# A two-layer trunk on one core: weights split in half tiles, and the first S5 scan issued behind the first SSD chunk

## The chip, the core and the metric

The kernel runs on one core of a Trainium2 chip. The metric is the device time of one execution in microseconds (us). The core has a matrix engine (TensorE, PE in the profile), three engines that work on tiles (VectorE or DVE, ScalarE or ACT, GpSimd or POOL), and SyncE (SP), whose queue issues all of this kernel's transfers. Tiles lie in SBUF with 128 partitions; matmuls write to PSUM. The three runs of the kernel before took 910.59, 910.69 and 911.84 us; the median is 910.69.

## The reference

The reference is a trunk of two layers on a sequence of 512 rows with 1024 columns, in fp32. Layer 0 runs two mixers side by side, and their inputs come from one projection:

```
hn = rmsnorm(h, layer_norm_w[i])
p = h @ w_in                       # gate S5 | gate SSD | S5 input u | SSD x,B,C | SSD dt
y_a = s5_mixer(u, ...)  * silu(z_a)
y_b = rmsnorm(ssd_mixer(xbc, dt, ...) * silu(z_b), ssd_norm_w, SSD_GROUPS)
h = h + concat(y_a, y_b) @ w_out
```

The S5 mixer is a diagonal complex state of 64 entries for each of 64 groups of 16 channels, `x_t = A x_(t-1) + B u_t`, with `y = C x + D u`, a GELU and a GLU. The SSD mixer has a causal depthwise convolution of width 4 over x, B and C, a SiLU, and then a chunked scan with chunks of 128 rows: within a chunk `y_diag = (C B^T * decay) (x dt)`, between chunks a state for each head that is carried on with a decay, and `y_off` from the carried state. Layer 1 is a chunkwise retention with four heads (q, k, v, gate), a group norm and an output projection. At the end stands an RMSNorm.

## The kernel before

**Projections.** Activations lie transposed, as eight tiles of 128x512 (eight slices of the 1024 inputs). A product with a weight tile of 128x1024 gives 128 output columns for all 512 rows. `ld_w` (L95) loads such a tile with one transfer into a `raw` buffer (three of them), and `split_w` (L101) makes two tiles of it: ACT copies it in a rounded form to `wh` (L107), and DVE subtracts that from the raw tile to `wl`, the low part (L108). There are two buffers each of `wh` and `wl`. In the trace the tile of a weight `z0` is called z0w when raw, z0h and z0l when split. `mm3` (L111) sums three products for each of the eight slices: high part by high input (L115), high part by low input (L116), low part by high input (L117), 24 matmuls in all. Some early tiles are used unsplit: `ld_raw` (L203) puts them in turn in a buffer of `raw`, `wh` and `wl`.

**Layer 0.** Its stages are x (SSD projection and conv), u (S5 input projection), z (gate projection), s (an SSD chunk: decays, states), t (the outputs of that chunk), and for the S5 mixer, in four parts j: l (load), g (state tables), a (scan), b (kernel tables), k (taps), c (outputs). The string `ORDER` (L36) sets the order in which these are written, and with it the priority of their instructions. A scheduler then orders each engine's queue by priority and readiness; weight splits (`rank_w`) and steps that free a PSUM bank (`rank_e`) have ranks of their own, and `tc.issue_after(x)` keeps an instruction behind x.

- The conv of tile m takes the PSUM sum of its projection through an ACT copy (L354) and three DVE steps (L357, tile cva), then a SiLU on ACT (L359). The last DVE step frees the PSUM bank, of which there are three for projections.
- The S5 input: ACT writes u to the tile us (L275), SP stores it to DRAM as `u_d` (L278), and `s5_load` reads two such tiles back in another layout as U (L730). The two of part 1 are us2 and us3, and U1 is read from them.
- A scan, `s5_scan`: PE forms the input sums S from the tables tm and al and from U (L755); DVE multiplies them by the rotation table rot (L767, L768, to the tiles gi and X), adds (L770), scans (L772), rotates back (L775, L777) and adds again (L782, to X and mg). rot is built by POOL (L534 to L539).
- Kernel tables, `s5_kern`: POOL multiplies and adds the tables O (L798, L802), and SP stores them to `o_d` (L803). Taps, `s5_taps`: PE forms K, ACT copies it to ks (L817), and DVE adds the feed-through on 16 columns for each half (L819).
- Outputs, `s5_out`: PE sums Y from Or (O read back) by X (L844) and from T (ks read back) by U (L845).
- An SSD chunk c with its two groups, `ssd`: transposes px, DVE products xdt (L385) and xds (L390), PE states st, DVE yos (L399) from the carried state, and the decays dec: read back from DRAM (L402), ACT Abs (L405) and Exp (L406), DVE product (L407). `ssd_y` uses yos, dec and xdt on PE (L425, L428).
- The gates z are stored to DRAM and read back later (zb2r is such a tile); the first group-norm sum over them is rsg0ps (L168).

**Layer 1** is made of projections by `ld_w` and `mm3` (or the same three products with the weights as moving operand, for v), and of the retention steps between.

## Time and profile before

| | |
|---|---|
| median of three runs | 910.69 us |
| the profiled execution | 915.33 us |
| its span in the trace | 913.6 us |
| mean granted clock of PE | 0.975 |
| PE busy | 868.6 us (95%) |
| DVE busy | 542.5 us (59%) |
| ACT busy | 359.5 us (39%) |
| POOL busy | 229.3 us (25%) |

The profiled execution is 4.64 us longer than the median. An engine's share of the span is a mean over both layers; layer 0 takes the first half of the span, layer 1 the second. In the trace's timeline a row has the start and the length of an instruction, or of several of one kind in a row, the engine, the line and the tiles, and in brackets the idle time just before it and what ended it. A row with `SPq` is SP issuing a transfer. The granted clock is given as a share of 2.4 GHz.

### The profile page before, as it was taken

Reading aid. Unit: us, or ns where it says so; the run is one execution under the profiler, and the core shown is the slowest. Engines: PE = TensorE matmul, PEld = TensorE weight load, DVE = VectorE, ACT = ScalarE, POOL = GpSimd, SP = SyncE. Lnnn points to the kernel's source line nnn. Section 1 sums busy time; section 2 is a strip of 40 time slices with the busy share of each in tenths; the row PEclk is TensorE's granted clock in tenths of the full one; section 3 lists DMA queues with packets and bytes.
Section 4 is the critical chain, followed back from the end, with each engine's and each line's share of the span. In section 5 each row is a group of like instructions: output and inputs, shape, how many; then the busy total and the mean of one; then the engine's idle time right before and its main releaser. Section 6 shows DMA issues by size and latency. Waiting matters only on the chain.

```text
span 913.6 us, 11520 instructions
## 1 busy us (share of the span) xinstructions
PE 868.6 (95%) x4348; PEld 683.1 (75%) x4348; DVE 542.5 (59%) x922; ACT 359.5 (39%) x572; POOL 229.3 (25%) x187
## 2 busy tenths in 40 slices
PE   8999955989989899999999999999999999999996
PEld 4345744757768787888888888888888888888885
DVE  6978769894883466453444544655633644448445
ACT  4323344425216444433434244345411244254432
POOL 0069997170572500000013122201000303110020
PEclk9999977979999899999999999999999999999999
DMA  7386313756549636773543221221332221222322
GB/s 244 122 223 210 106 51 119 204 161 205 148 124 323 215 104 190 255 238 107 208 141 112 93 93 47 93 92 47 99 103 99 93 91 47 93 70 70 116 70 93
DMA packets 64184, 121.45 MB, mean 133 GB/s; under 512 B 18112, under 2 KB 28672, under 8 KB 64000
## 3 DMA queue, kind: packets, MB, share of 16 engines
q1 hardware_dynamic: 64128, 120.71, 41.2%
q8 instruction: 34, 0.56, 0.2%
q14 instruction: 22, 0.18, 0.1%
HBM read 103.61 MB, written 17.07 MB: 132 GB/s over the span
## 4 chain that ended last, share of the span: by engine, by line
PE 68%; DVE 12%; POOL 8%; DMA 5%; SPq 2%; issue 2%; ACT 1%; ACTq 0%; POOLq 0%; DVEq 0%
PE g L115 3%; PE qk L117 3%; PE qk L116 3%; PE g L117 3%; PE g L116 3%; PE qk L115 3%; PE v L930 3%; PE v L931 3%; PE v L929 3%; PE gl L116 2%; PE gl L117 2%; PE gl L115 2%; PE out L117 2%; PE oa L116 2%; PE oa L117 2%
## 5 line engine op out<-in xcount | busy, mean ns | idle before, releaser
L903 POOL TENSOR_TENSOR rt<-rt,ru 128x512 f32<-128x512 f32 x16 | 27.2, 1721 | 134.7 <-DVE ru L902 134.7
L972 POOL TENSOR_TENSOR os<-os,os 128x512 f32<-128x512 f32 x12 | 15.5, 1292 | 139.8 <-ACT os L970 106.9
L882 POOL TENSOR_TENSOR hs<-hs,hs 128x512 f32<-128x512 f32 x7 | 12.0, 1708 | 92.5 <-ACT hs L880 92.5
L798 POOL TENSOR_TENSOR O<-ct,s5pws 128x512 f32<-128x512 f32 x16 | 24.1, 1508 | 31.2 <-DMA ct<-in_s5c_dram 31.2
L405 ACT ACTIVATE dec<-dec,nacs 128x128 f32<-128x128 f32 x64 | 19.5, 388 | 29.3 <-DMA dec<-at_d 29.3
L902 DVE TENSOR_TENSOR ru<-qk,tab 128x512 f32<-128x512 f32 x16 | 10.9, 683 | 32.4 <-PE qk L117 32.4
L357 DVE SCALAR_TENSOR_TENSOR cva<-xbc,cvw,cva 128x511 f32<-128x511 f32 (+2 forms) x36 | 26.6, 740 | 4.3 <-ACT cva L354 4.0
L798 POOL TENSOR_TENSOR ot<-ct,s5pws 128x512 f32<-128x512 f32 x16 | 28.1, 1756 | 0.0
L802 POOL TENSOR_TENSOR O<-O,ot 128x512 f32<-128x512 f32 x16 | 27.3, 1736 | 0.0
L742 POOL TENSOR_TENSOR tm<-al,b 128x512 f32<-128x512 f32 x6 | 9.0, 1513 | 57.3 <-DMA b<-in_s5bP_dram 34.2
L461 POOL TENSOR_TENSOR za6r<-za6r,y 128x512 f32<-128x512 f32 x1 | 1.3, 1297 | 80.9 <-DMA h_d<-hb 80.9
L359 ACT ACTIVATE cva<-cva 128x512 f32<-128x512 f32 x12 | 7.6, 631 | 33.7 <-DVE cva L357 33.6
L1004 DVE TENSOR_TENSOR h<-h,out 128x512 f32<-128x512 f32 x8 | 5.5, 686 | 25.5 <-PE out L117 25.5
L1065 POOL TENSOR_TENSOR fin<-fin,fnw 128x512 f32<-128x512 f32 x4 | 5.1, 1301 | 58.7 <-ACT fq L1029 58.7
L535 POOL TENSOR_TENSOR s5rt<-rot,s5lv 128x512 f32<-128x512 f32 (+4 forms) x7 | 5.9, 837 | 50.7 <-DVE s5lv L677 50.7
L845 PE MATMUL Y<-T,U 128*64 128x128 f32 x128 | 17.4, 294 | 0.2 <-issue 0.2
L499 DVE TENSOR_TENSOR hb<-ob,hb 128x512 f32<-128x512 f32 x8 | 5.5, 689 | 20.1 <-PE ob L117 20.1
L528 DVE TENSOR_TENSOR h<-oa,h 128x512 f32<-128x512 f32 x8 | 5.5, 690 | 19.6 <-PE oa L117 19.6
L848 ACT ACTIVATE ysb<-Y 128x256 f32<-128x256 f32 x16 | 5.2, 379 | 30.2 <-PE Y L845 18.1
L844 PE MATMUL Y<-Or,X 128*64 128x128 f32 x64 | 13.7, 298 | 2.3 <-DMA Or<-o_d 2.3
L120 ACT ACTIVATE rh<-rt 128x512 fp32r<-128x512 f32 (+1 forms) x16 | 9.1, 577 | 16.9 <-POOL rt L903 16.9
L425 PE MATMUL y<-ident,yos 128*128 128x128 f32 x48 | 12.2, 339 | 3.8 <-DVE yos L399 3.8
(1726 smaller groups left out, 3012.4 us busy)
## 6 DMA issues: line engine op xcount, KB each, us to landing
al<-al_d SPq DMA_DIRECT2D x8, 512.0 KB
b<-in_s5bP_dram SPq DMA_DIRECT2D x8, 512.0 KB
dec<-at_d SPq DMA_DIRECT2D x8, 512.0 KB
o_d<-O SPq DMA_DIRECT2D x16, 256.0 KB
T<-kd SPq DMA_DIRECT2D x64, 64.0 KB
Or<-o_d SPq DMA_DIRECT2D x16, 256.0 KB
x<-in_xT_dram SPq DMA_DIRECT2D x8, 256.0 KB
u_d<-us SPq DMA_DIRECT2D x8, 256.0 KB
```

Source lines behind the costliest of these rows:

```text
L115: pe.matmul(ps, wh[:, k, :], xh[k], start=start and i == 0, stop=False)
L116: pe.matmul(ps, wh[:, k, :], xl[k], start=False, stop=False)
L117: pe.matmul(ps, wl[:, k, :], xh[k], start=False, stop=stop and i == len(ks) - 1)
L357: vec.scalar_tensor_tensor(g[:, d:], ps[:, 0:SEQ - d], cvw[:, m, j:j + 1], g[:, d:], op0=ALU.mult, op1=ALU.add)
L405: act.activation(dec[:, i, :], dec[:, i, :], AF.Abs, bias=nacs[:, c, 8 * gr + i:8 * gr + i + 1])
L798: pool.tensor_tensor(x.rearrange("p (g k c) -> p g k c", g=4, c=16), ct[:, c, par, 4 * hf:4 * hf + 4].unsqueeze(2).broadcast_to(sh), pws[: ...
L802: pool.tensor_tensor(o, o, tm, op=ALU.add)
L845: pe.matmul(dst, U[:, 8 * par + 4 * hf + i, :], Tp[hf][:, 2 * i + par, :], start=False, stop=True)
L903: pool.tensor_tensor(t1, t1, t2, op=op)
L929: pe.matmul(ps[c], hh[kk][:, cs], wh[:, i, :], start=kk == 0, stop=False)
L930: pe.matmul(ps[c], hh[kk][:, cs], wl[:, i, :], start=False, stop=False)
L931: pe.matmul(ps[c], hl[kk][:, cs], wh[:, i, :], start=False, stop=kk == KD - 1)
```

## The change

Four things are changed.

1. Split weights are kept as two half tiles of 128x512 each for the high and the low part (names with 0 and 1 at their end), with four buffers each in place of two whole ones. ACT and DVE split each half with an instruction of its own. `piece` picks the half for a slice. The early unsplit tiles that lie in `wh` or `wl` buffers come in two transfers of 256 KB. The v projection and the second `on` projection of layer 1 use the halves as lists, in hunks left out here.
2. In `ORDER`, the first scan (a0) stands behind the first SSD chunk (s0), and its products by rot are issued behind the chunk's second xds.
3. The Exp of the decays is issued behind the last conv SiLU.
4. In the taps, ACT copies only the columns from 16 on, and DVE's feed-through reads the first 16 from PSUM.

```diff
-ORDER = """d0 x8 x10 x9 e0 x11 q0 x0 b0 x1 x2 w0 l0 g0 x3 x4 x5 x6 k0 b1 a0 x7 g1 s0 u2 u3 l1 t0 s1 z0 a1 z1 k1 b2 t1 s2 u4 c0 u5
+ORDER = """d0 x8 x10 x9 e0 x11 q0 x0 b0 x1 x2 w0 l0 g0 x3 x4 x5 x6 k0 b1 x7 g1 s0 a0 u2 u3 l1 t0 s1 z0 a1 z1 k1 b2 t1 s2 u4 c0 u5
...
-        return split_w(raw, name, halves)
-
-    def split_w(raw, name, halves=1):
-        h = wq.tile([P, KD, P], F32R, name=name + "h", tag="wh", bufs=2)
-        lo = wq.tile([P, KD, P], F32R, name=name + "l", tag="wl", bufs=2)
-        n = KD // halves
+        return split_w(raw, name)
+
+    KH = KD // 2
+
+    def w_half(name, tag, dt):
+        return wq.tile([P, KH, P], dt, name=name, tag=tag, bufs=4)
+
+    def split_w(raw, name):
+        hs, ls = [], []
         with rank_w():
-            for k in range(0, KD, n):
-                act.activation(h[:, k:k + n], raw[:, k:k + n], AF.Copy)
-                vec.tensor_tensor(lo[:, k:k + n], raw[:, k:k + n], h[:, k:k + n].bitcast(F32), op=ALU.subtract)
-        return h, lo
+            for i in range(2):
+                h, lo = w_half(f"{name}h{i}", "wh", F32R), w_half(f"{name}l{i}", "wl", F32R)
+                src = raw[:, i * KH:(i + 1) * KH]
+                act.activation(h, src, AF.Copy)
+                vec.tensor_tensor(lo, src, h.bitcast(F32), op=ALU.subtract)
+                hs.append(h), ls.append(lo)
+        return hs, ls
+
+    def piece(w, k):
+        return w[k // KH][:, k % KH]
 
     def mm3(ps, w, xh, xl, ks=range(KD), start=True, stop=True):
         wh, wl = w
         ks = list(ks)
         for i, k in enumerate(ks):
-            pe.matmul(ps, wh[:, k, :], xh[k], start=start and i == 0, stop=False)
-            pe.matmul(ps, wh[:, k, :], xl[k], start=False, stop=False)
-            pe.matmul(ps, wl[:, k, :], xh[k], start=False, stop=stop and i == len(ks) - 1)
+            pe.matmul(ps, piece(wh, k), xh[k], start=start and i == 0, stop=False)
+            pe.matmul(ps, piece(wh, k), xl[k], start=False, stop=False)
+            pe.matmul(ps, piece(wl, k), xh[k], start=False, stop=stop and i == len(ks) - 1)
 
...
-            raw = (wp if tag == "raw" else wq).tile([P, KD, P], F32, name=name + "w", tag=tag, bufs=3 if tag == "raw" else 2)
             wcount[0] += 1
             with rank(tc.cur_priority - ahead):
-                wdma[name] = sp.dma_start(raw, src).ins
-            return raw
+                if tag == "raw":
+                    raw = wp.tile([P, KD, P], F32, name=name + "w", tag="raw", bufs=3)
+                    sp.dma_start(raw, src)
+                    return raw[:, 0:KH], raw[:, KH:KD]
+                halves = []
+                for i in range(2):
+                    halves.append(w_half(f"{name}w{i}", tag, F32))
+                    sp.dma_start(halves[i], src[:, i * KH:(i + 1) * KH])
+                return halves
 
         def mm1(ps, raw, x):
             for k in range(KD):
-                pe.matmul(ps, raw[:, k, :], x[k], start=k == 0, stop=k == KD - 1)
+                pe.matmul(ps, piece(raw, k), x[k], start=k == 0, stop=k == KD - 1)
...
-            act.activation(g, g, AF.Silu)
+            held["silu"] = act.activation(g, g, AF.Silu).ins
...
-                        vec.tensor_tensor(xds.rearrange("p (h d) -> p h d", d=64), ps_x.rearrange("p (h d) -> p h d", d=64),
-                                          ds[:, c, hs].unsqueeze(2).broadcast_to([P, 8, 64]), op=ALU.mult)
+                        s5.setdefault("fed", []).append(
+                            vec.tensor_tensor(xds.rearrange("p (h d) -> p h d", d=64), ps_x.rearrange("p (h d) -> p h d", d=64),
+                                              ds[:, c, hs].unsqueeze(2).broadcast_to([P, 8, 64]), op=ALU.mult).ins)
...
-                act.activation(dec, dec, AF.Exp, scale=-1.0)
+                with tc.issue_after(held["silu"]):
+                    act.activation(dec, dec, AF.Exp, scale=-1.0)
...
-            vec.tensor_tensor(gi[c][:, :, 1:], sc, rot[:, 0, g8, 1:], op=ALU.mult)
-            vec.tensor_tensor(gt[1 - c][:, :, 1:], sc, rot[:, 1, g8, 1:], op=ALU.mult)
+            with tc.issue_after(s5["fed"][1]):
+                vec.tensor_tensor(gi[c][:, :, 1:], sc, rot[:, 0, g8, 1:], op=ALU.mult)
+                vec.tensor_tensor(gt[1 - c][:, :, 1:], sc, rot[:, 1, g8, 1:], op=ALU.mult)
...
-        act.activation(ks.rearrange("p g l -> p (g l)"), ps_k[:, 0:256], AF.Copy)
+        pk = ps_k[:, 0:256].rearrange("p (g l) -> p g l", g=2)
+        act.activation(ks[:, :, 16:], pk[:, :, 16:], AF.Copy)
         for hf in range(2):
             vec.scalar_tensor_tensor(ks[:, hf, 0:16], s5["eye"], s5["dK"][:, 2 * j + hf:2 * j + hf + 1],
-                                     ks[:, hf, 0:16], op0=ALU.mult, op1=ALU.add)
+                                     pk[:, hf, 0:16], op0=ALU.mult, op1=ALU.add)
```

On DVE, around the first scan, the order before was this. The number after cva is the conv tile; in gi00 and X01 the first digit is the part, in xdt00, xds00 and dec00 the SSD chunk.

```order
L357 SCALAR_TENSOR_TENSOR cva6_895<-xbc6_864,cvw_225,cva6_895 128x510
L766 MEMSET gi00_986 128x8
L767 TENSOR_TENSOR gi00_986<-S00_949,rot_502 128x8x63
L768 TENSOR_TENSOR X01_989<-S00_949,rot_502 128x8x63
L766 MEMSET gi01_987 128x8
L745 TENSOR_TENSOR al10_1045<-al10_1045,b10_1046 128x512
L761 MEMSET mg0_983 128x8
L743 TENSOR_TENSOR tm10_1047<-tm10_1047 128x512
L745 TENSOR_TENSOR al10_1045<-al10_1045,b10_1046 128x512
L357 SCALAR_TENSOR_TENSOR cva6_895<-xbc6_864,cvw_225,cva6_895 128x509
L767 TENSOR_TENSOR gi01_987<-S01_950,rot_502 128x8x63
L768 TENSOR_TENSOR X00_988<-S01_950,rot_502 128x8x63
```

In the order after, these rows stand there; cva6 and the u3 splits stand ahead of them.

```order
L406 TENSOR_TENSOR xds00_1056<-px00_1050,dcd_241 128x512
L372 SCALAR_TENSOR_TENSOR cva7_1012<-xbc7_977,cvw_227,cva7_1012 128x511
L372 SCALAR_TENSOR_TENSOR cva7_1012<-xbc7_977,cvw_227,cva7_1012 128x510
L372 SCALAR_TENSOR_TENSOR cva7_1012<-xbc7_977,cvw_227,cva7_1012 128x509
L424 TENSOR_TENSOR dec00_1060<-dec00_1060,cbn0_1043 128x1024
L113 TENSOR_TENSOR z0l0_1333<-z0w_1330,z0h0_1332 128x512
L424 TENSOR_TENSOR dec01_1085<-dec01_1085,cbn0_1043 128x1024
L400 TENSOR_TENSOR xdt01_1074<-px01_1075,dtn_238 128x512
L113 TENSOR_TENSOR z0l1_1337<-z0w_1330,z0h1_1336 128x512
L406 TENSOR_TENSOR xds01_1081<-px01_1075,dcd_241 128x512
L785 TENSOR_TENSOR gi00_1136<-S00_1099,rot_510 128x8x63
L786 TENSOR_TENSOR X01_1139<-S00_1099,rot_510 128x8x63
```

The first scan product moved from in front of the last step of cva6 to behind cva7, the z0 splits and both groups of SSD chunk 0.

On SP, the transfers up to U1 were issued in this order before.

```order
L821 DMA kd_578<-ks0_918 256x1x128
L803 DMA o_d_615<-O100_925 128x512
L803 DMA o_d_615<-O101_931 128x512
L98 DMA u4w_1566<-in_w_u_dram 128x1024
L803 DMA o_d_615<-O110_937 128x512
L803 DMA o_d_615<-O111_943 128x512
L278 DMA u_d_229<-us2_1157 128x512
L98 DMA u5w_1684<-in_w_u_dram 128x1024
L278 DMA u_d_229<-us3_1191 128x512
L730 DMA U1_1194<-u_d_229 128x16x64
```

After, they stand like this.

```order
L840 DMA kd_586<-ks0_946 256x1x128
L755 DMA al11_1029<-al_d_489 128x1x1024
L756 DMA b11_1030<-in_s5bP_dram 128x1024
L98 DMA u4w_1614<-in_w_u_dram 128x1024
L821 DMA o_d_623<-O100_953 128x512
L821 DMA o_d_623<-O101_959 128x512
L821 DMA o_d_623<-O110_965 128x512
L821 DMA o_d_623<-O111_971 128x512
L293 DMA u_d_231<-us2_1193 128x512
L98 DMA u5w_1736<-in_w_u_dram 128x1024
L293 DMA u_d_231<-us3_1231 128x512
L747 DMA U1_1234<-u_d_231 128x16x64
```

The transfers from O100 to U1 kept their places among one another; u4w moved ahead of them, and the loads al11 and b11 stand behind the taps' store.

On PE, before, the outputs y11 of SSD chunk 1 stood among the first sums of u5.

```order
L844 MATMUL Y00_1627<-Or00_1599,X00_988 64x128
L845 MATMUL Y00_1627<-T00_1607,U0_729 64x128
L117 MATMUL u5_1683<-xh0_697,u5l_1687 128x512
L115 MATMUL u5_1683<-xh1_701,u5h_1686 128x512
L116 MATMUL u5_1683<-xl1_702,u5h_1686 128x512
L117 MATMUL u5_1683<-xh1_701,u5l_1687 128x512
L115 MATMUL u5_1683<-xh2_705,u5h_1686 128x512
L116 MATMUL u5_1683<-xl2_706,u5h_1686 128x512
L425 MATMUL y11_1481<-ident_82,yos11_1273 128x128
L428 MATMUL y11_1481<-dec11_1275,xdt11_1260 64x128 x2
```

After, y10 comes first behind the last sums of u5 and one of z2 on PE.

```order
L124 MATMUL u5_1735<-xh7_737,u5h1_1742 128x512
L409 MATMUL st11_1309<-xds11_1307,cbn1_1265 128x512
L412 MATMUL yo11_1311<-prev1_1097,cva11_369 128x512
L125 MATMUL u5_1735<-xl7_738,u5h1_1742 128x512
L126 MATMUL u5_1735<-xh7_737,u5l1_1743 128x512
L124 MATMUL z2_1882<-xh0_709,z2h0_1885 128x512
L442 MATMUL y10_1512<-ident_82,yos10_1284 128x128
L445 MATMUL y10_1512<-dec10_1286,xdt10_1271 64x128 x2
```

So all 24 sums of u5 moved in front of y10. Behind the rest of y10, PE goes on like this in the order after.

```order
L863 MATMUL Y00_1679<-Or00_1651,X00_1138 64x128
L864 MATMUL Y00_1679<-T00_1659,U0_741 64x128
L863 MATMUL Y00_1679<-Or01_1653,mg0_1133 64x128
L864 MATMUL Y00_1679<-T00_1659,U0_741 64x128
L863 MATMUL Y00_1679<-Or00_1651,X00_1138 64x128
L864 MATMUL Y00_1679<-T00_1659,U0_741 64x128
L442 MATMUL y11_1529<-ident_82,yos11_1313 128x128
L445 MATMUL y11_1529<-dec11_1315,xdt11_1300 64x128 x2
```

Four more sums of Y than before stand between y10 and y11, and 17 more sums of u5 and z2 stand ahead of y11.

## Rows read from the trace of the kernel before

**Rows 1.** Windows: start:end, length, busy us of PE, PEld, DVE, ACT, POOL, clock, DMA share, GB/s.

```profile
153.70:158.60 4.90, 4.88 (x12) 3.84 (x13) 4.82 (x6) 0.00 (x0) 1.09 (x1) 0.51 0.52 161
...
196.00:207.00 11.00, 10.79 (x64) 7.79 (x64) 9.26 (x14) 4.43 (x12) 2.79 (x2) 0.53 0.88 290
...
140.00:160.00 20.00, 10.16 (x35) 7.35 (x34) 19.83 (x17) 8.18 (x10) 14.71 (x8) 0.74 0.38 124
500.00:600.00 100.00, 100.00 (x473) 84.09 (x472) 50.89 (x88) 34.29 (x50) 19.29 (x13) 1.00 0.25 84
...
159.20:164.20 5.00, 5.00 (x45) 3.78 (x43) 3.03 (x6) 2.14 (x3) 0.00 (x0) 1.00 0.99 260
```

**Rows 2.** Waits of PE: what it waited for, us, times, longest.

```profile
PE z L117 <- DVE z0l L108: 7.8, 1, 7.8
...
PE u L115 <- DVE cva L357: 5.2, 1, 5.2
...
PE u L117 <- DVE u3l L108: 4.2, 1, 4.2
...
PE z L115 <- DVE cva L357: 2.1, 1, 2.1
```

**Rows 3.** Timeline of DVE: start, us, instruction, idle before it.

```profile
113.86 2.04 DVE L819 SCALAR_TENSOR_TENSOR ks<-eye,dK,ks 128x16 f32<-128x16 f32 x2
...
120.78 0.68 DVE L767 TENSOR_TENSOR gi<-S,rot 128x504 f32<-128x504 f32 x1 [4.21 <-POOL rot L536]
124.31 0.68 DVE L768 TENSOR_TENSOR X<-S,rot 128x504 f32<-128x504 f32 x1 [2.85 <-POOL rot L539]
...
128.82 0.73 DVE L357 SCALAR_TENSOR_TENSOR cva<-xbc,cvw,cva 128x509 f32<-128x509 f32 x1
...
151.49 2.17 DVE L108 TENSOR_TENSOR z0l<-z0w,z0h 128x1024 fp32r<-128x1024 f32 x1
...
168.92 0.69 DVE L385 TENSOR_TENSOR xdt<-px,dtn 128x512 f32<-128x512 f32 x1 [1.18 <-PE px L383]
...
194.35 0.69 DVE L399 TENSOR_TENSOR yos<-yo,dcd 128x512 f32<-128x512 f32 x1
...
341.48 0.38 DVE L819 SCALAR_TENSOR_TENSOR ks<-eye,dK,ks 128x16 f32<-128x16 f32 x2
```

**Rows 4.** Timeline of PE: u2's first and last sum, S10, y11, the group-norm sum.

```profile
118.74 0.48 PE L115 MATMUL u<-xh,u2h 128*128 128x512 f32 x1
...
124.06 0.39 PE L117 MATMUL u<-xh,u2l 128*128 128x512 f32 x1
...
166.87 0.68 PE L755 MATMUL S<-U,tm 128*64 128x64 f32 x8
...
195.10 0.49 PE L425 MATMUL y<-ident,yos 128*128 128x128 f32 x2 [3.75 <-DVE yos L399]
...
303.37 0.38 PE L168 MATMUL rsg0ps<-ones,zb2r 128*128 128x1 f32 x2 [2.41 <-ACT zb2r L475]
```

**Rows 5.** Timeline of ACT: us2.

```profile
140.49 0.57 ACT L275 ACTIVATE us<-u 128x512 f32<-128x512 f32 x1
```

**Rows 6.** Timeline of POOL: the last two adds of the tables O of part 1.

```profile
143.65 3.38 POOL L802 TENSOR_TENSOR O<-O,ot 128x512 f32<-128x512 f32 x2
```

**Rows 7.** Timeline of SP's queue: us2, us3, U1, and later zb2r.

```profile
147.47 0.38 SPq L278 DMA_DIRECT2D u_d<-us  x1
...
154.12 0.38 SPq L278 DMA_DIRECT2D u_d<-us  x1
158.15 0.37 SPq L730 DMA_DIRECT2D U<-u_d  x1
...
285.83 0.37 SPq L471 DMA_DIRECT2D zb2r<-z_d  x1
```

**Rows 8.** One line's instructions: min/median/max ns, first and last start; half and whole tile.

```profile
L121 DVE TENSOR_TENSOR xl<-xn,xh x8: 680/687/1639, 32.9 to 85.7; 128x512 fp32r<-128x512 f32 x8
...
L108 DVE TENSOR_TENSOR z3l<-z3w,z3h x1: 1224/1224/1224, 213.4 to 213.4; 128x1024 fp32r<-128x1024 f32 x1
```

More of the change, by code (lines that the diff above doesn't have):

```diff
@@ L93, in rank_e, with ld_w @@
         return rank(-1000000 + 20 * wcount[0])
-    def ld_w(src, name, halves=1, ahead=0):
+    def ld_w(src, name, ahead=0):
         raw = wp.tile([P, KD, P], F32, name=name + "w", tag="raw", bufs=3)
@@ L248, in layer0 @@
             for k in range(KD):
-                pe.matmul(pu[0], w0[0][:, k, :], xs[k], start=k == 0, stop=k == KD - 1)
+                pe.matmul(pu[0], piece(w0[0], k), xs[k], start=k == 0, stop=k == KD - 1)
             y0, last = root(sq[:1], D, "rs0"), held0[0]
@@ L1033, in layer1 @@
         for kq in range(4):
-            wh, wl = (q.rearrange("p k m -> p (k m)").rearrange("p (i n) -> p i n", n=512)
+            wh, wl = ([x.rearrange("p k m -> p (k m)") for x in q]
                       for q in ld_w(a["w_o1b"][0, kq].rearrange("p i (j m) -> p (i j) m", m=P), f"on{kq}"))
```

14 lines of the change are left out of this document (7 added, 7 removed).

## The prediction

> **What bounds the kernel now.** The windows come first: they show where TensorE (PE) is not working. From 500 to 600 us it is busy for all of the 100 us at full clock, with DVE at 51 and ACT at 34; from 140 to 160 it works for 10.16 of 20 us at a mean clock of 0.74, while DVE is busy for 19.83 [rows 1]. So layer 1 is limited by PE alone, and nothing that the change does to DVE, ACT or SP is worth anything there, as long as they stay under PE. What can be won lies in layer 0, where PE waits. The list of waits names its releasers there: z0's low-part weights 7.8 us, two conv results 5.2 and 2.1, u3's low part 4.2, together 19.3 us [rows 2].
>
> All four end on DVE, so DVE's own timeline is read next. DVE stood still for 4.21 us until 120.78 and for 2.85 more until 124.31, in front of the first scan's two products, which wait for a POOL table (rot) [rows 3]. In that queue stand, behind the products, the last conv tap of cva6 (128.82), which frees the PSUM bank that u3 wants, and, behind the whole scan, z0l at 151.49. The scan's output is not wanted by PE before the Y sums near 189. That is why PE stands: DVE spends 7.1 us idle and some 20 us on work that is early.
>
> **The order, part by part.** The scan moves behind the second xds of SSD chunk 0. By the order after, cva6, u3l, xdt00, xds00, cva7, dec00, z0l and dec01 all stand in front of the first scan product, and none of them reads the POOL table. POOL's table was complete when the 2.85 us wait ended at 124.31, and the sixteen or so DVE instructions that now stand ahead of the scan last beyond that, so no wait replaces the 7.1 us. The dec Exps wait for the last Silu; they are read by dec00's product only, and one table load instead of three is seen by ACT, which has idle time there. On ACT nothing that PE needs soon is queued behind that wait: z0h and us2 stand ahead of it or come while it is open. I take the four waits as gone except for about 2 us of z0's, so PE could reach its next fixed point, the first S sum of the second half (S10, 166.87 [rows 4]), 17.2 us earlier, at 149.7.
>
> **The wait that takes their place.** S10 reads U1, and U1 does not come earlier by as much. Its chain: us2 is ready on ACT at 141.06 (140.49 + 0.57) [rows 5], but its transfer stands on SP behind the four o_d transfers, and the last of those waits for POOL's add that ends at 147.03 (143.65 + 3.38) [rows 6]. So SP issued us2 at 147.47, then u5w, then us3 at 154.12, then U1 at 158.15, 4.03 us behind us3 [rows 7]. In the order after, the same chain stands on SP: O100 to O111, us2, u5w, us3, U1. What goes is the delay of us3 from 147.9 to 154.12, since u5w took a buffer that z0 held and no longer does. So us2 at 147.5, us3 at 148.3, U1 at 152.3. For its landing no row gives a time: between 4.0 (a transfer of half the size, us3, by U1's issue behind it) and 8.7 (S10 began so long after the issue without waiting). DMA carried nothing from 158 to 159 and then 260 GB/s for 5 us [rows 1], at which 0.5 MB with T's pieces behind it take some 3 to 4; I take 5, nearer to the first end. S10 then starts at 157.3 (156.3 to 161) in place of 166.87. (The Trainium skill, page "DMA: Bandwidth & Descriptors", section "Anatomy of one DMA — SWDGE (gpsimd) path", gives some 2.0 us fixed for each transfer and 436 GB/s on top: an estimate of 3.2 us for U1, by which S10 would start at 155.5 and 10.9 us would be won here. By that rule us3, of half the size, would need 2.6; the row's 4.03 says otherwise, and I stay with the row.) Two of the ten z1 sums that stood ahead now stand behind, 24 sums from 118.74 to 124.06 being 0.23 us apart [rows 4]: 0.46. Won at this place: 9.57 - 0.46 = **9.1 us**, of 17.2 removed; PE waits there for some 8 to 15 us.
>
> PE's clock: in 153.7 to 158.6, right after the 7.8 us wait, it was 0.51, and in 196 to 207, after a wait of 3.75, it was 0.53, so the lower of its two levels (1.2 GHz, not 2.4) nearly all along [rows 1]. After the new wait I expect a slow stretch of the same length: 4.9 x 0.49 = 2.4 at least, 5 at most (11 x 0.47, the other row); I take 2.8. Before paid one here too, but upstream of S10, inside the 166.87.
>
> **The next point, y11.** y11 started at 195.10, after waiting 3.75 us for yos11, which DVE began at 194.35 [rows 3, 4]. Before S10 to y11 is 28.2 us, 24.5 of it work. The order after puts 17 more projection sums ahead of y11 (16 of u5, one of z2: 3.9 us) and 4 more Y sums (0.4): the place that answers to 195.10 is 199.4. PE's side: 157.3 + 24.5 + 4.3 + 0.5 (z1) + 2.8 (clock) = 189.4. DVE's side: its xdt10 at 168.92 came 2.05 behind S10's start; at 157.3 + 2.05 + 1.0 for the slow clock it comes at 160.3, and the 25.4 us to yos11 carry over. Added: z2l and z3l's first half, 3 x 0.68 = 2.0 [rows 8], a product X that was earlier, 0.7; more slow PE sums that DVE waits for, 1.8; more time beside POOL, 1.5. Less: 1.7 for the taps (below). So yos11 begins at 190.0 to 192.6, say 191, and y11 0.75 behind it at 191.8: a wait of 2.4 us remains, and the gain is 199.4 - 191.8 = **7.6 us**. That wait is near the old one, so the slow stretch behind it is taken as unchanged.
>
> **The taps.** The two ks products took 2.04 us beside POOL (113.86) and 0.38 alone (341.48) [rows 3]. With K read from PSUM they have one SBUF tensor less. The conv taps, which also read PSUM, took 0.73 at 128.82 while POOL worked, so I take 0.38: 1.7 saved on DVE each time POOL works beside it, bounds 0 and 1.7 (at 0, yos11 and with it the end come 1.7 later). ACT's copy becomes shorter by 16 of 128 columns, worth nothing.
>
> **Half tiles.** A half takes 0.68 on DVE where a whole tile took 1.22 [rows 8]: 0.14 more a tile, and some more on ACT, which has more room. In layer 1 that lies under PE (51 of 100 us on DVE). In layer 0 ten tiles before y11 make 1.4 us on DVE, of which those in DVE's chain are in the sum already. PE may start on a first half some 0.7 us sooner where it waits for a low part; that is within the 2 us that I left of z0's. The early raw weights come in two transfers of half the size: one SP issue more each, about 0.35 by SP's rows [rows 7], hidden behind the transfers; bounds minus 0.5 and plus 0.5.
>
> **After y11.** The next waits of PE in layer 0 are short ones and are taken with their sizes, moved with everything else. The doubtful one is the first group-norm sum, 2.41: it began at 303.37 when ACT had zb2r [rows 4], a transfer that SP issued at 285.83 [rows 7], at the end of a chain of u, U and z_d transfers whose start is a scan on DVE. It moves only if that scan does.
>
> **Sum.** The profiled execution took 915.33 us, 4.64 above the median of 910.69; the terms are differences and so are carried to the median: 910.69 - 7.6 = **903.1**, I say 903.
>
> **Rivals.**
> A, the forecast: U1's arrival takes the place of the four waits, and half of the gain reaches the end. 900 to 906, chance 0.50.
>
> B, more: yos11 comes before PE does (DVE's collisions with POOL are smaller than I add, or U1 lands 1 us sooner), the wait at y11 goes, and with it the slow stretch behind, whose 11 us at 0.53 cost 5.2 [rows 1]. 7.6 + 5.2 gives 897.9; with the later waits shorter too, 894. For it: the margin is only 2.4 us. Against: U1's wait is as long a stop as the ones that go, and a stop has each time brought a slow clock. Chance 0.22.
>
> C, slower: the chain to zb2r does not move. By the order the first group-norm sum stands behind 16 of z8's 24 sums, where all of z8 and two of z9 were in front: 10 sums, 2.3 us, less work to fill the wait. If zb2r leaves ACT no sooner than before, just ahead of 303.37 in the profiled time, PE arrives 7.6 us early, waits, and starts all that follows at the old time plus 2.3: 913.0. It decides from the point at which the DMA chain gains less than 2.3 us. Against: all of the chain's starts stand behind DVE's first and second scans or behind PE sums that come earlier, but its middle is DMA at near full share. Chance 0.10.
>
> D, given back in part: POOL's O chain is held up by DVE, which is now busy where it idled (120 to 125), so U1 is issued later; each us there is a us off the 9.1. The new company is at most the 7.1 us in which DVE idled; if POOL took twice as long in them, U1 came 7 us later and 0.5 to 1 us of the gain would be left: 909 to 910.5. Against: the scan that stood beside POOL's O products before is now behind them, and the pair of ks shows DVE, not POOL, being held (2.04 against 0.38) [rows 3]. Chance 0.18 for a loss of over 3 us, of which 0.10 within the bound below.
>
> That nothing moves is excluded: the order after has the scan behind z0l.
>
> **How the numbers follow.** Of differences, 0.2% (1.8 us) is about what a measurement of this kernel can tell from no change: 908.9 and 912.5. Slower is C, 0.10. Same is the end of D, 0.10. Faster is A, B and the rest of D, 0.80. The range reaches from B's lower end, 894, to 909.5, which leaves out C, most of D's end, and little below.
>
> **What would show it.** Right: no idle DVE at 116 to 124; PE's four waits replaced by one of 8 to 15 us in front of S, released by U1's transfer, ended near 157; a slow clock right behind it; ks near 0.4 for the pair; one wait of about 2 us at y11; the group-norm wait no longer than 3 us. Wrong: S starts after 162 (POOL or SP was late, D); y11 has no wait and the clock stays up (B); the group-norm wait grows to 8 or more (C). If PE waits for U1 less than 5 us, my reading of what removes the four waits is wrong, whatever the total says.

## The result and the profile after

The changed kernel took 899.16 us (three runs, 898.78 to 900.46) against 910.69 before: a ratio of 0.987 with a 95% interval of 0.9835 to 0.9905, so 8.7 to 15.0 us less. The forecast was 903, with a range of 894 to 909.5. In a second measurement, on another chip beside the experiments, the same kernel took 900.97 us against 912.42, a ratio of 0.9867 (0.9841 to 0.9894). The profiled execution shown here took 898.78 us.

The waits of PE after the change (what it waited for, us, times, longest) answer to [rows 2]:

```profile
PE st L409 <- DVE xds L406: 13.7, 1, 13.7
PE y L442 <- DVE yos L415: 5.1, 1, 5.1
...
PE S L772 <- DMA U<-u_d: 1.1, 1, 1.1
...
PE rsg0ps L177 <- ACT zb2r L492: 0.8, 1, 0.8
```

All four waits of [rows 2], 19.3 us, are gone. One of 13.7 us stands in their place, and it is not the one for U1. In PE's timeline it stands ahead of two places of [rows 4]: S1, the input sums of part 1 (S10 in the prediction is the first of them), and y11:

```profile
136.15 2.05 PE L409 MATMUL st<-xds,cbn 128*128 128x512 f32 x2 [13.74 <-DVE xds L406]
...
158.00 0.56 PE L772 MATMUL S<-U,tm 128*64 128x64 f32 x6 [1.09 <-DMA U<-u_d]
...
194.45 0.67 PE L442 MATMUL y<-ident,yos 128*128 128x128 f32 x2 [5.07 <-DVE yos L415]
...
291.68 0.38 PE L177 MATMUL rsg0ps<-ones,zb2r 128*128 128x1 f32 x2 [0.83 <-ACT zb2r L492]
```

What PE waited for at 136 is read from DVE's timeline, which answers to [rows 3]:

```profile
109.38 0.36 DVE L838 SCALAR_TENSOR_TENSOR ks<-eye,dK,K 128x16 f32<-128x16 f32 x2
...
122.69 3.07 DVE L759 TENSOR_TENSOR tm<-al,b 128x512 f32<-128x512 f32 x2 [12.29 <-POOL rot L556]
125.69 0.73 DVE L372 SCALAR_TENSOR_TENSOR cva<-xbc,cvw,cva 128x509 f32<-128x509 f32 x1
...
135.33 0.68 DVE L406 TENSOR_TENSOR xds<-px,dcd 128x512 f32<-128x512 f32 x1
...
149.37 0.67 DVE L785 TENSOR_TENSOR gi<-S,rot 128x504 f32<-128x504 f32 x1
...
165.75 0.69 DVE L400 TENSOR_TENSOR xdt<-px,dtn 128x512 f32<-128x512 f32 x1
...
193.71 0.69 DVE L415 TENSOR_TENSOR yos<-yo,dcd 128x512 f32<-128x512 f32 x1
```

DVE still stands in front of POOL's rotation table, now for 12.29 us in one piece where it was 7.06 in two. The instruction that waits does not read the table: it is the first product of the state tables of the second part, tm10. Behind it stand the last conv step of cva6, the u3 splits and the xds at 135.33 for which PE waits. The first scan's product, at 149.37, waits for nothing any more.

SP's queue, which answers to [rows 7]: us2, the load of u5w, us3 and U1:

```profile
145.26 0.32 SPq L293 DMA_DIRECT2D u_d<-us  x1
148.87 0.33 SPq L98 DMA_DIRECT2D u5w<-in_w_u_dram  x1
149.30 0.38 SPq L293 DMA_DIRECT2D u_d<-us  x1
153.61 0.37 SPq L747 DMA_DIRECT2D U<-u_d  x1
```

The windows say where the time went. Columns as in [rows 1]: PE's idle time is the length less PE's busy time. The kernel before:

```profile
100.00:200.00 100.00, 76.98 (x494) 57.57 (x492) 84.88 (x95) 38.77 (x76) 73.10 (x49) 0.88 0.42 126
200.00:400.00 200.00, 191.89 (x1212) 153.75 (x1211) 117.88 (x181) 87.61 (x145) 47.90 (x32) 0.96 0.65 203
```

The kernel after, in the first measurement and then in the second:

```profile
100.00:200.00 100.00, 79.28 (x522) 61.34 (x521) 82.72 (x109) 38.74 (x84) 67.89 (x48) 0.89 0.43 132
200.00:400.00 200.00, 198.63 (x1255) 158.62 (x1254) 127.83 (x205) 91.94 (x170) 49.51 (x33) 0.99 0.66 212
400.00:880.00 480.00, 480.00 (x2236) 402.46 (x2235) 252.36 (x458) 201.22 (x352) 53.45 (x39) 1.00 0.28 94
```

```profile
100.00:200.00 100.00, 79.56 (x525) 61.37 (x524) 83.13 (x111) 38.59 (x84) 67.53 (x48) 0.86 0.44 135
200.00:400.00 200.00, 197.69 (x1229) 158.01 (x1229) 125.04 (x199) 90.61 (x168) 48.88 (x33) 0.96 0.65 206
```

From 100 to 200 us, where the change was made, PE idles 20.7 us (20.4) in place of 23.0: only 2.3 to 2.6 us less. From 200 to 400 it idles 1.4 us (2.3) in place of 8.1: 5.8 to 6.7 us less. From 400 on it is busy throughout, with the half tiles too. Most of the idle time that went in these windows was not where the change's first scan is, but where I had taken the waits as unchanged.

**A measure without the clock.** The two executions of the changed kernel in these fences have nearly the same idle time, and their spans are 897.0 and 901.7 us; what differs most is the granted clock, 0.983 against 0.974. So for each kernel the span times the granted clock is given beside the time below (the mean over the runs, with its standard error): the span that the same execution would have had if PE's clock had always been full, roughly. The rest, span times one less the clock, is called the clock's share. It is rough because a wait at the low clock counts half in it: in the first execution of the changed kernel PE stood idle at a clock of 0.50 from 126.4 to 136.0 us, and 4.8 us of that wait are booked to the clock. For the kernel before it was 888.0, 888.3 and 888.3 us on the three chips of the experiments (plus or minus 0.3 to 0.6), and the clock's share 21 to 22.

| kernel | runs | median us | ratio to before (95%) | span x clock | clock's share |
|---|---|---|---|---|---|
| changed kernel, second measurement | 6 | 900.97 | 0.9867 (0.9841 to 0.9894) | 881.0 ± 0.8 | 18.4 ± 1.3 |
| whole tiles | 10 | 907.67 | 0.9955 (0.9931 to 0.9979) | 885.2 ± 0.6 | 20.5 ± 0.7 |
| scan in front | 10 | 909.98 | 0.9983 (0.9958 to 1.0008) | 885.7 ± 0.5 | 22.4 ± 0.6 |
| without the small parts | 6 | 899.58 | 0.9861 (0.9829 to 0.9894) | 879.0 ± 0.4 | 19.5 ± 0.9 |
| scratch table elsewhere | 9 | 905.21 | 0.9927 (0.9892 to 0.9961) | 883.9 ± 0.6 | 19.1 ± 0.8 |
| the same, U1 in front | 10 | 908.16 | 0.9955 (0.9924 to 0.9987) | 884.6 ± 0.6 | 21.1 ± 0.8 |
| tables late | 6 | 900.07 | 0.9860 (0.9832 to 0.9888) | 878.4 ± 0.9 | 19.9 ± 1.0 |
| tables late, U1 in front | 6 | 903.55 | 0.9900 (0.9870 to 0.9929) | 881.2 ± 0.7 | 20.7 ± 1.0 |
| two instructions, whole buffers | 6 | 899.47 | 0.9872 (0.9845 to 0.9900) | 881.4 ± 0.6 | 16.9 ± 1.3 |
| tables late, without the small parts | 12 | 908.46 | 0.9964 (0.9942 to 0.9986) | 884.4 ± 0.3 | 22.6 ± 1.0 |
| POOL's tables behind yos11 | 6 | 900.66 | 0.9885 (0.9860 to 0.9909) | 881.8 ± 0.6 | 17.7 ± 0.6 |
| the three together | 12 | 909.08 | 0.9983 (0.9961 to 1.0006) | 884.1 ± 0.7 | 23.5 ± 0.9 |

One run of the kernel with the scratch table elsewhere, of 913.44 us, was in a slow state and is left out of the table. By this measure the gain of the changed kernel is some 7 us, with some 4 more booked to the clock (22.4 to 18.4, standard errors 1.0 and 1.3). PE's idle time over the whole span, in the first execution of each kernel, fell by 9.7 us, from 45.0 (span 913.6, busy 868.6) to 35.3 (897.0, 861.7). The experiments ran on three chips in groups of four, in the order of the sections below; the ratio is each time to the kernel before on the same chip.

### The profile page after: what moved, and what is told of

Same layout as the page of the kernel before. It is cut to its first block, busy times and chain, and to the rows that moved or that the text cites. A ratio compares the mean times of both kernels' runs of the same rounds, so it can differ in the third digit from the quotient of the medians.

```text
span 897.0 us, 11872 instructions
## 1 busy us (share of the span) xinstructions
PE 861.7 (96%) x4348; PEld 679.7 (76%) x4348; DVE 554.8 (62%) x1033; ACT 376.5 (42%) x681; POOL 217.6 (24%) x187
## 4 chain that ended last, share of the span: by engine, by line
PE 75%; POOL 10%; DVE 8%; DMA 3%; issue 2%; ACT 1%; SPq 1%; POOLq 0%; ACTq 0%; DVEq 0%
PE g L124 3%; PE qk L126 3%; PE qk L125 3%; PE qk L124 3%; PE g L126 3%; PE g L125 3%; PE v L949 3%; PE v L948 3%; PE v L950 3%; PE z L126 2%; PE z L125 2%; PE z L124 2%; PE ob L124 2%; PE ob L125 2%; PE ob L126 2%
## 5 line engine op out<-in xcount | busy, mean ns | idle before, releaser
L922 POOL TENSOR_TENSOR rt<-rt,ru 128x512 f32<-128x512 f32 x16 | 23.8, 1504 | 136.2 <-DVE ru L921 136.2
L901 POOL TENSOR_TENSOR hs<-hs,hs 128x512 f32<-128x512 f32 x7 | 9.1, 1294 | 95.4 <-ACT hs L899 95.4
L421 ACT ACTIVATE dec<-dec,nacs 128x128 f32<-128x128 f32 x64 | 19.5, 391 | 15.3 <-DMA dec<-at_d 15.1
L816 POOL TENSOR_TENSOR ot<-ct,s5pws 128x512 f32<-128x512 f32 x16 | 25.7, 1609 | 0.0
L759 DVE TENSOR_TENSOR tm<-al,b 128x512 f32<-128x512 f32 x10 | 10.7, 1112 | 19.9 <-POOL rot L556 12.3
L409 PE MATMUL st<-xds,cbn 128*128 128x512 f32 x12 | 7.3, 690 | 13.7 <-DVE xds L406 13.7
L759 POOL TENSOR_TENSOR tm<-al,b 128x512 f32<-128x512 f32 x6 | 8.1, 1368 | 39.6 <-PE z L125 20.4
L442 PEld LDWEIGHTS y<-ident,yos 128*128 128x128 f32 x48 | 8.0, 205 | 9.9 <-DVE yos L415 5.3
L424 DVE TENSOR_TENSOR dec<-dec,cbn 128x1024 f32<-128x1024 f32 x8 | 11.5, 1437 | 5.2 <-ACT dec L423 5.1
L130 DVE TENSOR_TENSOR rl<-rt,rh 128x512 fp32r<-128x512 f32 (+1 forms) x16 | 14.2, 906 | 0.7 <-ACT rh L129 0.6
```

The lines of the kernel that those rows point to most:

```text
L421: act.activation(dec[:, i, :], dec[:, i, :], AF.Abs, bias=nacs[:, c, 8 * gr + i:8 * gr + i + 1])
L442: pe.matmul(ps_y[:, pr * P:(pr + 1) * P], yo[:, pr * P:(pr + 1) * P], ident, start=True, stop=False)
L816: pool.tensor_tensor(x.rearrange("p (g k c) -> p g k c", g=4, c=16), ct[:, c, par, 4 * hf:4 * hf + 4].unsqueeze(2).broadcast_to(sh), pws[: ...
L922: pool.tensor_tensor(t1, t1, t2, op=op)
```

## The experiments

**Half tiles undone.** The other three parts stay.

```diff
-                h, lo = w_half(f"{name}h{i}", "wh", F32R), w_half(f"{name}l{i}", "wl", F32R)
...
+        h, lo = w_whole(name + "h", "wh", F32R), w_whole(name + "l", "wl", F32R)
         with rank_w():
+            act.activation(h, raw, AF.Copy)
+            vec.tensor_tensor(lo, raw, h.bitcast(F32), op=ALU.subtract)
```

> The changed kernel with whole weight tiles again (two buffers each, one ACT copy and one DVE subtraction a tile); the other three parts of the change stay. Theory (the scan's move carries the gain): 899 to 902 us, and of the later waits of the kernel before the one on z4's low part (1.6 us) comes back. Rival (the half tiles carry it, by letting PE start on the first half): 905 us or more, with a wait of several us on a low part.

It took 907.67 us, 6.7 over the changed kernel's second measurement (8 by the two ratios to before, since the chips differ): the rival's side, by more than the theory allowed. The two windows, and the wait that matters from PE's timeline, with SP's row for what it waited for:

```profile
100.00:200.00 100.00, 83.14 (x547) 63.66 (x547) 80.65 (x106) 40.14 (x85) 70.10 (x49) 0.90 0.48 145
200.00:400.00 200.00, 189.63 (x1192) 152.05 (x1189) 115.91 (x172) 83.66 (x136) 53.41 (x33) 0.97 0.64 201
```

```profile
257.51 0.66 PE L857 MATMUL Y<-Or,X 128*64 128x128 f32 x2 [6.13 <-DVE z4l L110]
...
258.52 0.80 PE L120 MATMUL u<-xh,u7h 128*128 128x512 f32 x1
```

```profile
254.41 0.32 SPq L841 DMA_DIRECT2D Or<-o_d  x1
```

From 200 to 400 us PE idles 10.4 us, where the changed kernel idles 1.4 to 2.3. The wait is 6.13 us, in front of the second half of the Y sums of part 1. The profile puts it down to z4l, but these sums do not read z4l. They read Or, and SP could issue that transfer only at 254.41, when DVE's third scan had just written mg (252.73 + 1.66 = 254.39), so Or's arrival is the likely end of the wait. In the changed kernel the same transfer went out at 254.22 and the same sums began at 258.07: their gate did not move. What differs is PE's order. With whole tiles, 12 of u7's 24 sums, whose weights were ready, and all of z4 stand behind these Y sums. In the changed kernel all of u7 and the first three sums of z4 stand in front of them, and PE does not wait:

```profile
257.30 0.39 PE L124 MATMUL z<-xh,z4h 128*128 128x512 f32 x1
...
258.07 0.43 PE L863 MATMUL Y<-Or,X 128*64 128x128 f32 x2
```

**The scan undone.** The first scan stands again in front of the SSD chunk; half tiles, late exponentials and taps stay.

```diff
- ... k0 b1 x7 g1 s0 a0 u2 u3 ...
+ ... k0 b1 a0 x7 g1 s0 u2 u3 ...
-            with tc.issue_after(s5["fed"][1]):
-                vec.tensor_tensor(gi[c][:, :, 1:], sc, rot[:, 0, g8, 1:], op=ALU.mult)
+            vec.tensor_tensor(gi[c][:, :, 1:], sc, rot[:, 0, g8, 1:], op=ALU.mult)
```

> The changed kernel with the first scan back in front of the SSD chunk, in the order string and without the condition on the second xds; half tiles, late exponentials and taps from PSUM stay. Theory (the scan's move carries the gain): 907 to 911 us, the waits on cva, u3's and z0's low parts return. Rival (half tiles and late exponentials carry it): 903 us or less.

It took 909.98 us, and its ratio to before reaches 1. The waits of PE, and the two windows:

```profile
PE y L442 <- DVE yos L415: 6.3, 1, 6.3
PE u L126 <- DVE u3l L113: 5.6, 1, 5.6
PE st L409 <- DVE xds L406: 4.6, 2, 3.9
...
PE z L124 <- DVE cva L372: 2.2, 1, 2.2
```

```profile
100.00:200.00 100.00, 77.54 (x494) 57.96 (x492) 80.86 (x100) 38.12 (x84) 64.75 (x47) 0.93 0.41 122
200.00:400.00 200.00, 197.01 (x1227) 157.09 (x1228) 119.89 (x206) 89.20 (x166) 51.86 (x35) 0.93 0.65 208
```

The early waits are back in changed shape (22.5 us idle from 100 to 200), while the later ones stay away (3.0 idle from 200 to 400, where the kernel before has 8.1). In PE's idle time from 100 to 200 and from 200 to 400 us, the kernel before has 23.0 and 8.1, with the scan's move alone it is 16.9 and 10.4, with the half tiles alone 22.5 and 3.0, with both 20.7 and 1.4. So the half tiles act after 200, with or without the move. The scan's move acts before 200, but by 6.1 us with whole tiles and only 1.8 with half tiles; over both windows it is worth 3.9 and 3.4. The time hides the half tiles' effect here, since the clock was low from 200 on (0.93 in this profile, and the largest clock's share but two of the table). By span times clock each part is worth 4 to 5 us in the presence of the other, 2 to 3 alone, and both together 7.

**The scratch table elsewhere.** Is DVE's 12.29 us a wait for the table, or for its scratch buffer? In the built program tm10 waits for a semaphore of POOL in the changed kernel and for one of PE in the kernel before. The state tables take their buffers in turn from a ring of eight, and POOL's scratch tile s5rt lies in that ring too. Here it is put elsewhere.

```diff
-        rt = f("s5rt", [P, 2, 32, 16])
+        rt = tp.tile([P, 2, 32, 16], F32, name="s5rt", tag="g", bufs=3)
```

> The changed kernel with one edit: the scratch tile s5rt of POOL's rotation table lies in a buffer of the decay tiles and not in the ring of buffers that the state tables (al, b, tm) use. Theory (DVE's new wait of 12.3 us on POOL's table at tm10 is a wait for a buffer, and it makes PE's 13.7 us): that wait and PE's on xds go, PE then waits for U1 as I forecast, S1 begins near 154.5 where it began at 158.0, and the total is 893 to 897 us. Rival (the wait is covered by U1 anyway): 899 plus or minus 1.

DVE's wait is gone, so it was a wait for the buffer. But with one tile fewer in the ring DVE made the second part's state tables early, from 81.85 us on, among the first convs, and PE waits there instead:

```profile
PE y L442 <- DVE yos L415: 5.8, 1, 5.8
...
PE xbc L229 <- issue: 2.6, 1, 2.6
...
PE xbc L124 <- DVE cva L372: 2.3, 1, 2.3
```

S1 began at 157.04 us, although u2 began 8 us later than in the changed kernel. With 905.21 us the theory's 893 to 897 is missed: one edit of a ring moved too much to tell the price of the wait. The next group therefore moved the waiting instruction alone.

**The scratch table elsewhere, and U1 in front of the o_d writes.**

```diff
- ... k0 b1 x7 g1 s0 a0 u2 u3 l1 t0 ...
+ ... k0 x7 g1 s0 a0 u2 u3 l1 b1 t0 ...
```

> As the kernel with the scratch tile elsewhere, and the second part's kernel tables (b1) stand behind u3 and U1's load in the order string, so that on SP the writes of us2 and us3 and the load of U1 no longer stand behind the four o_d writes that wait for POOL. Theory (U1's arrival is the next bound at S1): S1 begins at 147 to 150, 5 to 8 us sooner than with the tile alone; about half of that is left behind the wait on yos11, so 889 to 894 us. Rival (POOL's tables, now later, are waited for at the taps or at the Y sums): no faster than with the tile alone, with a wait on K, Or or O.

U1 was issued at 147.65, 6 us sooner than in the changed kernel, but S1 began at 159.71, later than with the scratch table alone, and the time was 908.16 us. PE's list has no wait for U1 left; just in front of S1 stand 4.54 us put down to the SSD outputs on DVE. The theory that U1 is the next bound fell for this order.

**The tables late.** The state tables of the second part are written behind the scan, and tm10 is issued behind the first xds. On DVE these rows move to behind xds00.

```diff
- ... b1 x7 g1 s0 a0 u2 ...
+ ... b1 x7 s0 a0 g1 u2 ...
+            with (tc.issue_after(s5["fed"][0]) if (j, par) == (1, 0) else nullcontext()):
                 for c in range(2):
                     eng.tensor_tensor(tm[:, c], al[:, c], b[:, c], op=ALU.mult)
```

> The changed kernel with one edit: the state tables of the second part (g1) are written behind the scan, and DVE's first product of them (tm10) is issued behind the first xds, so that the conv, the u3 splits and the xds no longer stand behind the wait for POOL's rotation table. Theory (that wait of 12.3 us on DVE makes PE's 13.7 us): PE's wait on xds goes or falls under 3 us, and z0 begins some 10 us earlier than 146.0; S1 then waits for U1, whose chain over ACT is shorter, and begins at 154 to 157; total 2 to 5 us under the changed kernel on this chip. Rival (U1 and then yos11 give all of it back): within 1.5 us of the changed kernel, the wait only moved.

DVE's and PE's timelines around it:

```profile
122.70 3.10 DVE L760 TENSOR_TENSOR tm<-al,b 128x512 f32<-128x512 f32 x2 [7.02 <-POOL rot L556]
```

```profile
133.28 0.47 PE L398 MATMUL px<-ident,cva 128*128 128x128 f32 x1 [5.31 <-ACT cva L374]
141.85 0.50 PE L126 MATMUL z<-xh,z0l 128*128 128x512 f32 x1 [1.48 <-DVE z0l L113]
151.32 0.56 PE L773 MATMUL S<-U,tm 128*64 128x64 f32 x6 [1.61 <-DMA U<-u_d]
155.06 0.66 PE L391 MATMUL pb<-ident,cva 128*128 128x128 f32 x2 [3.18 <-DVE cva L449]
```

PE's wait of 13.74 us is gone, so it came from tm10. (tm10 itself still waits for POOL, 7.02 us, though the scan is written ahead of it again.) The cva7 steps still stand behind tm10, and PE waits 5.31 for their result. S1 begins at 151.32, 6.7 us earlier than in the changed kernel, and waits for U1 for 1.61; y11 begins at 187.16, with a wait of 1.20. Yet the time is 900.07 us against 900.97, the rival's outcome by its bound: PE then waits for DVE in front of SSD chunk 2 (2.75 us at 193.56) and idles 4.2 us after 200, and the clock's share is higher. Span times clock is 2.6 us lower, with a standard error of 1.2. Whether a small gain is left can't be told from six runs.

**The tables late, and U1 in front.** The same move of b1 as above.

> As the kernel with the tables late, and the kernel tables b1 stand behind u3 and U1's load, so that us2, us3 and U1 pass the o_d writes on SP. Theory (U1 is the next bound at S1): S1 begins at 146 to 150; y11 then waits longer for yos11, since DVE's work does not shrink; total 1 to 4 us under the kernel with the tables late alone. Rival (POOL's later tables are waited for by K or Or, or DVE bounds y11 wholly): the same or slower than with the tables late alone.

S1 began at 151.33, not earlier. us2 went out at 140.26 where it was 141.68, and us3 at 141.78 where it was 142.65, but U1 followed us3 after 5.2 us where it was 4.4, so that it was issued at 147.00 for 147.08. us2 and us3 come from ACT at 140.2 and 141.8 there: behind POOL's tables, ACT is the next gate, less than 2 us away. y11 waited 8.7 us for yos11 and began at 196.85. At 903.55 us it is no faster than with the tables late alone; the intervals overlap.

**Without the two small parts.** The exponentials are issued as before, and the taps read the copy.

```diff
-                with tc.issue_after(held["silu"]):
-                    act.activation(dec, dec, AF.Exp, scale=-1.0)
+                act.activation(dec, dec, AF.Exp, scale=-1.0)
...
-                                     pk[:, hf, 0:16], op0=ALU.mult, op1=ALU.add)
+                                     ks[:, hf, 0:16], op0=ALU.mult, op1=ALU.add)
```

> The changed kernel without its two small parts: the exponentials are issued as before, and the taps' feed-through reads the copy. Theory (they matter little): within 2 us of the changed kernel; two more table loads of 1.28 us on ACT. Rival (the late exponentials keep the copies of u2, u3 and z0 in time on ACT): 3 us or more slower, with a wait of PE on ACT or on a low part.

899.58 us, and PE's two long waits are the same (13.7 on xds, 4.7 on yos11). The two small parts are worth nothing that these runs can tell. The pair of ks, read from the copy, took 1.38 us here at 108.83.

The **changed kernel itself** ran in that group:

> The changed kernel itself, beside the kernel before on the same chip as the other experiments. If 899.16 holds for this chip too, the half tiles (907.67 without them) and the scan's move (909.98 without it) are each worth 8 to 11 us in the presence of the other. If it lies at 904 or above, the single kernels are closer to it than their difference from 899.16 says, and each is worth a few us only.

900.97 us: the first of the two cases by the time. By span times clock, each part is worth 4 to 5.

**Two instructions, whole buffers.** Do the half tiles win because a buffer's first half is free sooner, or because the split's instructions are shorter?

```diff
         h, lo = w_whole(name + "h", "wh", F32R), w_whole(name + "l", "wl", F32R)
         with rank_w():
-            act.activation(h, raw, AF.Copy)
-            vec.tensor_tensor(lo, raw, h.bitcast(F32), op=ALU.subtract)
+            for i in range(2):
+                k = slice(i * KH, (i + 1) * KH)
+                act.activation(h[:, k], raw[:, k], AF.Copy)
+                vec.tensor_tensor(lo[:, k], raw[:, k], h[:, k].bitcast(F32), op=ALU.subtract)
```

> The changed kernel with whole buffers again (two of 128x1024 each for high and low part), but still with two ACT copies and two DVE subtractions of half a tile each. Theory (the buffers carry the half tiles' gain: a first half is free when PE is through four of the eight slices, so the next weight's split gets ahead of a scan on DVE): about the time of the kernel with whole tiles, 904 to 909 us, with a wait of some us on a low part near 260. Rival (the shorter instructions carry it): 902 us or less, without that wait.

899.47 us: the rival. The copies of z4, by its line, first here and then in the changed kernel:

```profile
L111 ACT ACTIVATE z4h<-z4w x2: 616/624/633, 247.5 to 248.1; 128x512 fp32r<-128x512 f32 x2
```

```profile
L112 ACT ACTIVATE z4h<-z4w x2: 634/634/634, 238.6 to 248.9; 128x512 fp32r<-128x512 f32 x2
```

With half buffers the first copy does come 9 us sooner (238.6 against 247.5), and that was my theory's mechanism; but it is worth nothing that these runs can tell. What gains against the kernel with whole tiles is the split in two instructions alone: 7 to 8 us in time by the ratios, 3.8 (885.2 to 881.4) in span times clock. Here too all of u7 stands in front of the Y sums that waited 6.13 us. How it comes about is not shown: it may be that a product's first half depends on an instruction of its own, or that the scheduler, given shorter instructions, writes another order.

**Tables late, without the small parts.**

> Both single edits that came out level or better: the tables late, and without the two small parts. Theory (what each saved in waits adds up): span times granted clock falls to 877 or less from 881.0 of the changed kernel, and the time to 896 to 899 us. Rival (they remove the same waits, or the slow clock takes it back): 899 to 901 us.

908.46 us. Two edits that are level alone lose some 8 us together, by the ratios. PE's waits:

```profile
PE Y L862 <- DMA Or<-o_d: 7.3, 3, 4.4
PE S L772 <- DMA U<-u_d: 5.9, 1, 5.9
...
PE rsg0ps L177 <- ACT zb1r L491: 3.2, 1, 3.2
```

From 100 to 200 PE idles 14.9 us, where the changed kernel idles 20.7, and after 200 it idles 11.3, most of it for transfers: PE has got ahead of chains that did not move with it. Here U1 does bound S1, for 5.9 us.

**POOL's tables behind yos11.** The first product of the third part's tables is issued behind yos11.

```diff
+                with (tc.issue_after(s5["yo", 1, 1]) if j == 2 and hf + par == 0 else nullcontext()):
+                    for c, x in enumerate((o, tm)):
```

> The changed kernel with POOL's first product of the third part's kernel tables issued behind yos11, so that POOL does not work while DVE goes through the second scan. Theory (the wait of about 5 us at y11 is DVE slowed by POOL: its scan adds took 1.5 to 1.7 us there and 0.69 alone): DVE's scan steps fall to 0.7 each, the wait at y11 falls below 1 us, total 2 to 5 us under the changed kernel. Rival (the collisions only move to DVE's next work, or POOL's later tables are waited for): within 1.5 us or slower.

POOL's first product there, in this kernel and then in the changed one:

```profile
177.29 1.10 POOL L818 TENSOR_TENSOR O<-ct,s5pws 128x512 f32<-128x512 f32 x1 [27.59 <-DMA ct<-in_s5c_dram]
```

```profile
177.61 1.12 POOL L816 TENSOR_TENSOR O<-ct,s5pws 128x512 f32<-128x512 f32 x1 [27.61 <-DMA ct<-in_s5c_dram]
```

The edit moved nothing: POOL starts at the same time, 16 us ahead of yos11, so issuing behind an instruction of another engine added no wait here. So its 900.66 us say nothing on the question. How much of the wait at y11 is POOL beside DVE was not measured.

**The three together.**

> The three edits together: tables late, without the two small parts, POOL's tables behind yos11. Theory: if each removes its own wait, 893 to 897 us. Rival: as the best of the single ones, 898 to 900 us, because DVE's work between S1 and y11 bounds all of them.

909.08 us, as the pair of the tables and the small parts: the third edit did nothing here either. No version is clearly better than the changed kernel.

## Why the prediction was right or wrong

**The range held, and the median was 4 us under the forecast.** The direction was right, and the scan's move is a cause: without it the time is level with before. It is not the main one: with it alone, on whole tiles, the time is 0.9955 of before and not 0.987, and the half tiles, which I had costed at nothing, are worth as much. That the total fell into the range is partly luck: the gain up to y11 was 4.95 us for 7.6, and what came behind y11 made up for it.

**The four waits.** They went, as forecast. What failed is the sentence that no wait replaces the 7.1 us since nothing ahead of the scan reads POOL's table. I had read the new order, in which tm10 stands between the last two steps of cva6, but not what each instruction waits for. In the new order tm10's buffer in the ring was the one that POOL's scratch tile still held, and the wait grew from 7.06 to 12.29 us. Two experiments show it: with the scratch tile elsewhere the wait goes, and with tm10 behind the xds PE's 13.74 goes. Why the ring gave it that buffer was not shown: with the tables late the scan is written ahead of g1, as before, and tm10 still waits for POOL.

**S1 and U1.** The forecast was 147.5, 148.3 and 152.3 for the three transfers and 157.3 for S1; measured are 145.26, 149.30, 153.61 and 158.00 [rows 4, 7]. The landing, taken as 5 us, was 4.39 (153.61 to 158.00). The wait of 8 to 15 us that I put there was 1.09, since PE came late through the wait on xds. The sum itself gives 7.6 there (157.3 less 149.7; 6.6 to 11.3 by the bounds), and not 8 to 15. So the place was right by luck, by two chains that ended within 1.1 us of each other; my own condition for a wrong reading (under 5 us of waiting for U1) was met. That U1 was a close second shows where tm10 is moved away: S1 then comes 6.7 us earlier and waits 1.61, because us2 too had been held on ACT (145.23 in the changed kernel, 2.8 us behind the last o_d write) behind the same DVE work. One step of the chain failed: that z0 no longer holds u5w's buffer. SP issued u5w at 148.87, just when DVE ended the second z0l (147.67 + 1.17 = 148.84), so us3, ready on ACT at 147.28, went out behind it, 1.0 us later than forecast though us2 was 2.2 sooner. POOL's o_d writes, which I had as the gate, were not the gate that counted: moving them away brought S1 not forward at all, in two orders.

**y11.** Forecast 191.8 with a wait of 2.4, measured 194.45 with 5.07. PE's side came out: it was ready at 189.38 for 189.4. DVE's did not: yos11 began at 193.71 for 191. (The terms that I added up for it give 190.05; the step to 191 has no term.) Against the place that I worked out for the same work, 199.4, that is a gain of 4.95 and not 7.6. The term that failed is xdt10's distance from S1: 2.05 us was carried over from the kernel before, and it was 7.75 (165.75 less 158.00). The first scan's later steps, which used to lie ahead of S1, now lie between the two. The 30.7 us that I allowed from xdt10 to yos11 were 27.96.

**After y11.** Taken as unchanged, this was the largest error: PE's idle time there fell from 8.1 us to 1.4 and 2.3. The half tiles do it, which I had costed at nothing off the path (10.4 us idle there without them, 3.0 with them and without the scan's move). I looked only for waits on a low part, of which [rows 2] had few, and not at what PE's order puts into other waits.

**Taps, half tiles' length, the group norm.** The pair of ks took 0.36 us at 109.38, with POOL at work, for 2.04 [rows 3]; forecast 0.38. The end is not moved by it. The split in halves costs ACT and DVE more (DVE is busy 554.8 us for 542.5), and PE covers it from 400 us on as forecast. The group-norm sum's wait became 0.83 and not longer, so rival C did not come. Its mechanism did, in the kernel with the tables late and without the small parts: PE ahead, then 7.3 and 3.2 us on transfers.

**The clock.** The slow stretch after the new wait was forecast at 2.8 us; the clock was 0.50 from 136 to 140 us and 1.00 from 140 to 145, so some 2 us went. A slow stretch behind y11 was forecast to stay, and it did in the changed kernel:

```profile
195.00:200.00 5.00, 5.00 (x25) 3.29 (x25) 4.56 (x9) 0.00 (x0) 1.47 (x1) 0.50 0.88 254
```

Of rival B, which had the wait at y11 gone, nothing came; the time lies nearer to its 897.9 than to 903 by other causes, the later waits and some 4 us of the clock's share (18.4 against 22.4 on the same chip, standard errors 1.3 and 1.0). What made that share smaller was not shown; fewer waits after 200 us fit it, and so does chance in part.

## What to carry to other kernels

When code is written in another order, read what every moved instruction's neighbours wait for, not only where they stand: buffers taken in turn from a ring pass to other tiles, and here a wait of 12 us came from a scratch tile that nothing near it reads. Splitting an instruction that prepares an operand in two can pay where no wait names it: here other matmuls then stood in front of a late one and filled its wait. Whether the buffer is split as well mattered nothing here. A wait's named releaser may be an instruction whose result the waiting one does not read; look for what it does read. And two edits that were level alone lost 8 us together, so a pair is measured as a pair.
